# Two steps instead of three for a pair of attention heads, and both halves of the sample's scores at once

## The chip, the cores and the metric

The kernel runs as one program on one core of one Trainium2 chip. The metric is the time of one execution on the device in microseconds (us); the median of three runs of the kernel before is 1309.05 us (1308.57 to 1309.22). Engines are named as in the profile: PE is the matrix engine with its weight loads (PEld) beside it, DVE the vector engine, ACT the scalar engine with its function table, POOL the general engine, and SP the engine from whose queue the kernel starts its DMA transfers. PSUM is the memory that PE writes to; the other engines read it from there.

## The reference

One inference step of a two-layer encoder with a prompt of 512 frames (the rows 0 to 511) and a sample request of 32 frames (rows 512 to 543) that share the weights. Cut to what the change touches, with the shapes of this case (d_model 1024, 8 attention heads of 64, past of 256):

```python
def layer(x, ...):
    u = x @ w_in                       # 13 groups of columns: q, k, v, z of attention, of retention, ...
    # prompt: each chunk of 64 frames reads itself and the 8 chunks before it
    ya = band_attention_prompt(qa, ka, va, rel_table)
    # sample: 32 frames read 256 cached keys and their own 32
    ya = band_attention_sample(qa, ka, va, k_cache, v_cache, rel_table)
    ya = ya * silu(za)
    yb = group_norm_heads(retention(rope(qb), rope(kb), vb, ...)) * silu(zb)
    yc = rg_lru(xr, ...) * silu(zc)
    merged = sum(sigmoid(g_b) * (y_b @ w_branch[b]) for b in (A, B, C))
    r = ALPHA * x + merged @ w_out
    r = r + sigmoid(r @ w_ple_gate) * (pe @ w_ple)
    return layer_norm(r)

# both attentions, per head
scores = q * d**-0.5 @ k.T + rel_bias        # masked to the band for the prompt
probs = softmax(scores)
out = probs @ v
```

Since 8 chunks of 64 frames are the whole prompt but one chunk, a frame of the prompt reads all chunks up to its own: the scores of the four query tiles of 128 frames (i = 0 to 3) are 128, 256, 384 and 512 columns wide.

## The kernel before, in words

**The stream of blocks.** Activations lie with features on partitions and the 544 frames along the free axis. All large products are made of blocks: a 128x128 piece of a weight matrix against 544 frames, in two spans of 288 and 256 columns, and three times over, since both factors are split into a high and a low part (`xh`, `xl`, `wh`, `wl`); a block is so six matmuls at L256. Eight blocks (or four, or two) make a unit: an output tile, in one of two buffers of two PSUM banks each, that an evacuation (`evac`, lines 840 to 940) then copies or combines. A layer has 752 blocks, in the order of `layer_units()`: among others xr, va, then qa and ka in turn, kb, vb, qb, then za and what follows. Weights are loaded in chunks of eight blocks (`wr`, 3 buffers) and split into parts for four blocks at a time by ACT (`wh`, L211) and DVE (`wl`, L212), eight blocks ahead.

**What sets the order.** Everything else runs in generators, called jobs. `tick()` is called once ahead of each block; it issues the split that is due and then resumes every job whose time has come. A job says with `yield n` after how many blocks it wants to go on; these numbers stand in the table `PACE`. So the order of instructions on every engine is fixed when the program is built, and each engine and each DMA queue runs its list in order. If an instruction on PE waits for another engine, all blocks behind it wait with it.

**Attention of the prompt.** Once `ka` of head pair 0 is there, `attn_job` goes through the four pairs of heads. For a pair, three steps are added, 8 blocks apart: query tiles (0, 1), (2,) and (3,). A step (`attn_step`, L394 and on) takes the two buffers "sc" of PSUM (one bank of 512 columns each), one for each head j of the pair, and makes the scores by three products for each head and tile (high by high, low by high, high by low; L407). `exps` (L355 to L359) adds the bias and finds the row's extreme on DVE, takes the exponential on ACT with the row's sum; `norm` (L363, L364) multiplies by the reciprocal on DVE. Head 0's exponentials are issued with the scores, head 1's three blocks later together with head 0's norms, head 1's norms another three blocks later, and the transposes of head 0 two more (L423, by a matmul with the identity, 128 columns each, into the one "tp" bank); ACT copies them into `PT` (L429). Head 1's transposes follow three blocks behind. The product with V of a pair (`attn_pv`, L441, eight matmuls, in the one "pv" bank) is kept in a list and made by `flush()` right behind the first transposes of the next pair's step (0, 1); the last one comes `attn_end` = 9 blocks after the last step's slot. These pieces lie among the blocks of qa, ka, kb and vb.

**The sample.** `sample_job` starts behind `ka` of the last pair: it loads its cache and its biases `sb` (by SP, eight transfers), waits for "ya" (which stands from the first attention step on), and then 11 blocks. For j = 0 it makes scores (four matmuls at L468, 32 rows each at its own place in one bank), then exps; four blocks later the same for j = 1; the norms another four blocks later; then after four blocks the three transposes of j = 0 in the "tp" bank and two copies, and three blocks later those of j = 1; then three blocks later the product with V (L494).

**Behind attention.** `ret_job` starts once attention, the sample and the last tile of kb are there. It first turns VB (`flip`, L334: four transposes into "tp", then a copy), then KB, piece by piece. VB's tile t = 3 is copied out of PSUM by ACT (L866) at the end of its unit.

## Time and profile before

| what | value |
|---|---|
| median of the three runs | 1309.05 us (1308.57 to 1309.22) |
| profiled execution: time, span | 1308.99 us, 1307.2 us |
| granted PE clock in it | 0.997 of full speed |
| PE busy | 1290.2 us, 99% of the span |
| DVE, ACT, POOL busy | 719.6, 547.0, 176.3 us |
| PE on the chain that ended last | 95% of the span |

The profiled execution lies 0.06 us under the median. The span is the time from the first to the last recorded instruction; 1.8 us of the execution lie around it. In rows of the timeline the columns are: start in us from the span's start, length in us, engine, source line, operation, output and inputs, sizes and types, how many alike in a row, and in brackets the idle time of the engine before it with what ended it. "x2" behind a 288-column matmul stands for the pair of spans, 288 and 256.

### The profile page before, as it was taken

The page shows a single profiled execution, that of the slowest core. Times are in us where ns is not written, and L with a number is a line of the kernel's source. Part 1 is how long each engine was busy: PE and PEld are TensorE (multiplying, and loading weights), DVE is VectorE, ACT ScalarE, POOL GpSimd, SP SyncE. Part 2 cuts the span into 40 slices and gives each one's busy share as a digit, 9 for nine tenths or more (in the row PEclk, how much of TensorE's full clock was granted, in tenths as well). Part 3 has the DMA queues.
Part 4 walks back from the last instruction along what each step waited for, and adds up shares of the span by engine and source line. Part 5 has one row for each costly group of instructions (what it writes and reads, how often), then busy time and mean ns, then how long its engine had stood idle before and what let it go on. Part 6 is the DMA issues. An engine that isn't in the chain of part 4 may idle for free.

```text
span 1307.2 us, 25090 instructions
## 1 busy us (share of the span) xinstructions
PE 1290.2 (99%) x10552; PEld 1255.8 (96%) x10552; DVE 719.6 (55%) x1273; ACT 547.0 (42%) x1083; POOL 176.3 (13%) x158
## 2 busy tenths in 40 slices
PE   9999999999999999999999999999999999999996
PEld 9999889999999999999989998999999999999996
DVE  5666663563754443455584756626637534434567
ACT  6665544323632233323277655443235322332231
POOL 0210121410101101000032102125001011010000
PEclk9999999999999999999999999999999999999998
DMA  7333522321222222434132335222212222224231
GB/s 285 132 131 98 174 66 83 96 92 51 96 81 82 98 80 82 165 101 143 65 112 72 130 99 166 74 83 89 87 62 81 98 81 89 90 82 166 81 114 69
DMA packets 44609, 134.80 MB, mean 103 GB/s; under 512 B 9488, under 2 KB 11792, under 8 KB 42704
## 3 DMA queue, kind: packets, MB, share of 16 engines
q1 hardware_dynamic: 44496, 133.20, 30.6%
q8 instruction: 83, 1.36, 0.5%
q14 instruction: 30, 0.25, 0.1%
HBM read 117.02 MB, written 11.70 MB: 98 GB/s over the span
## 4 chain that ended last, share of the span: by engine, by line
PE 95%; DVE 3%; DMA 1%; ACT 1%; issue 0%; SPq 0%; POOL 0%; DVEq 0%
PE mm L256 84%; PE sc L407 2%; PE pv L441 1%; PE tp L423 1%; PE tp L334 1%; DMA raw<-in_W 1%; PE sc L667 1%; PE pv L690 1%; PE pv L522 0%; DVE r L819 0%; PE sc L522 0%; DVE xl L265 0%; PE sc L750 0%; PE sc L603 0%; PE pv L685 0%; PE sc L494 0%
## 5 line engine op out<-in xcount | busy, mean ns | idle before, releaser
L256 PE MATMUL mm<-xh,wh 128*128 128x288 f32 x2144 | 455.5, 294 | 0.4 <-ACT xrp L900 0.4
L256 PE MATMUL mm<-xh,wl 128*128 128x288 f32 x2144 | 444.2, 288 | 0.0
L256 PE MATMUL mm<-xl,wh 128*128 128x288 f32 x2144 | 442.8, 288 | 0.0
L212 DVE TENSOR_TENSOR wl<-raw,wh 128x512 fp32r<-128x512 f32 (+1 forms) x354 | 262.6, 760 | 282.3 <-ACT wh L211 277.2
L256 PEld LDWEIGHTS mm<-xh,wh 128*128 128x128 f32 x2144 | 328.4, 189 | 10.8 <-issue 7.5
L256 PEld LDWEIGHTS mm<-xl,wh 128*128 128x128 f32 x2144 | 328.8, 188 | 0.0
L256 PEld LDWEIGHTS mm<-xh,wl 128*128 128x128 f32 x2144 | 328.6, 188 | 0.0
L211 ACT CAST wh<-raw 128x512 fp32r<-128x512 f32 (+1 forms) x354 | 208.2, 614 | 36.0 <-PE mm L256 30.8
L922 ACT ACTIVATE sg<-mm 128x544 f32<-128x544 f32 x48 | 30.0, 625 | 154.0 <-PE mm L256 154.0
L934 POOL TENSOR_TENSOR m<-m,sg 128x544 f32<-128x544 f32 x30 | 46.8, 1561 | 316.7 <-DVE sg L932 316.7
L359 ACT ACTIVATE sx<-sx,sst 128x128 f32<-128x128 f32 (+4 forms) x68 | 38.0, 559 | 67.1 <-DVE sst L357 60.2
L256 PE MATMUL mm<-xh,held 128*128 128x288 f32 (+1 forms) x320 | 64.1, 292 | 0.3 <-ACT ple L942 0.3
L256 PE MATMUL mm<-mh,wh 128*128 128x288 f32 (+1 forms) x256 | 53.0, 288 | 0.0
L256 PE MATMUL mm<-mh,wl 128*128 128x288 f32 (+1 forms) x256 | 53.0, 288 | 0.0
L256 PE MATMUL mm<-ml,wh 128*128 128x288 f32 (+1 forms) x256 | 52.8, 287 | 0.0
L256 PEld LDWEIGHTS mm<-xh,held 128*128 128x128 f32 x320 | 51.3, 188 | 0.6 <-ACT ple L942 0.5
L256 PE MATMUL mm<-xl,held 128*128 128x288 f32 (+1 forms) x160 | 46.4, 290 | 0.6 <-DVE xl L265 0.6
L264 ACT CAST xh<-r 128x544 fp32r<-128x544 f32 (+2 forms) x32 | 17.0, 532 | 68.3 <-DVE r L952 64.1
L932 DVE TENSOR_TENSOR sg<-mm,sg 128x544 f32<-128x544 f32 x32 | 23.2, 725 | 37.0 <-PE mm L256 37.0
L913 ACT ACTIVATE z<-mm 128x544 f32<-128x544 f32 x24 | 15.0, 626 | 60.6 <-PE mm L256 60.5
L571 POOL TENSOR_TENSOR swap<-swap,cst 128x544 f32<-128x544 f32 x16 | 24.9, 1554 | 108.3 <-DMA swap<-QB 32.1
L256 PEld LDWEIGHTS mm<-mh,wh 128*128 128x128 f32 x256 | 39.4, 189 | 0.0
(251 smaller groups left out, 1783.4 us busy)
## 6 DMA issues: line engine op xcount, KB each, us to landing
raw<-in_W SPq DMA_DIRECT2D x189, 512.0 KB, 3.3
pled<-ple SPq DMA_DIRECT2D x4, 1088.0 KB, 9.8
ple<-pled SPq DMA_DIRECT2D x4, 1088.0 KB, 7.0
bias<-in_RB SPq DMA_DIRECT2D x16, 256.0 KB, 3.7
x<-in_xT SPq DMA_DIRECT2D x4, 544.0 KB, 9.5
o_v<-VA SPq DMA_DIRECT2D x2, 1088.0 KB, 4.6
o_k<-KT SPq DMA_DIRECT2D x2, 1088.0 KB, 5.1
swap<-KB SPq DMA_DIRECT2D x32, 68.0 KB, 2.0
```

The source lines that it names most:

```text
L211: S.copy(h[:, k:k + step], t)
L212: V.tensor_tensor(lo[:, k:k + step], t, h[:, k:k + step].bitcast(F32), SUB)
L256: T.matmul(ps[:, MM0 + a:MM0 + b], lhsT=w[:, n % 4, :], rhs=x[:, a:b], start=first and i == 0, stop=last and i == 2)
L264: S.copy(h, src)
L334: T.transpose(tp[:rows, t * 128:(t + 1) * 128], src[:, t, c0:c0 + rows], ident)
L359: S.activation(x, x, AF.Exp, bias=s[:, 0:1], scale=-1.0, accum_out=s[:, 1:2])
L407: T.matmul(scs[j][:, o:o + n], lhsT=q_[r, p, i * 128:i * 128 + 128], rhs=k_[r, p, :n], start=k == 0, stop=k == 2)
L571: G.tensor_tensor(sw, sw, cst[:, C_SIN:C_SIN + N], MUL)
L913: S.activation(z, pv, AF.Sigmoid)
L922: S.activation(sg, pv, AF.Sigmoid)
L932: V.tensor_tensor(sg, pv, sg, MUL)
L934: (V if kind == "bB" and t == 7 else G).tensor_tensor(m, m, sg, ADD)
```

## The change

**Attention.** A pair of heads takes two steps instead of three. The first ("wide") holds query tiles 3 and 1: tile 3's scores (512 columns) in the two "sc" banks as before, tile 1's (256 columns) in the "tp" bank for head 0 and in the "pv" bank for head 1. After the exponentials tile 1 of both heads lies side by side in a third buffer `x`. The second ("narrow") holds tiles 2 and 0, 384 and 128 columns, together in a head's "sc" bank. The wide step turns three full buffers with four transposes each (head 0's tile 3, head 1's tile 3, then tile 1 of both), the narrow one two; a wide step copies the first two with one instruction each, the third with two. `flush()` stands behind the wide step's first transposes. `PACE["step"]` becomes (11, 13), so that a pair still takes 24 blocks, and `attn_end` 3.

**The sample.** The loads of `sb` are moved behind the wait for "ya" and 14 blocks, with 12 blocks to the scores. Both halves' scores are made at once, in the two "sc" banks. All six transposes follow in one place, in two new "sc" banks: the four full ones in one, the two of 32 rows in the other; two copies take them out instead of four.

```diff
-    "va0": 5, "va": 3, "step": 8, "attn_end": 9, "at1": 3, "at2": 2, "at3": 3, "sample": 11, "sa1": 4, "sa2": 4,
+    "va0": 5, "va": 3, "step": (11, 13), "attn_end": 3, "at1": 3, "at2": 2, "at3": 3, "sample": 14, "sa1": 4, "sa2": 4,
...
-                for qs in ((0, 1), (2,), (3,)):
-                    if qs[0] == 2 and p < 3:
+                for n, qs in enumerate(((3, 1), (2, 0))):
+                    if n and p < 3:
                         bias_loads(p + 1)
                     add(attn_step(p, qs))
-                    yield PACE["step"]
+                    yield PACE["step"][n]
...
-            scs, xs, todo = [psum("sc") for _ in range(2)], [], []
-            o = 0
+
+            wide = qs[0] == 3
+            scs, xs = [psum("sc") for _ in range(2)], [tmp("sx", (128, 512)) for _ in range(2)]
+            at_ = {(qs[0], j): (scs[j], xs[j], 0) for j in range(2)}
+            if wide:
+                x = tmp("sx", (128, 512))
+                at_.update({(qs[1], j): (psum(("tp", "pv")[j]), x, 256 * j) for j in range(2)})
+            else:
+                at_.update({(qs[1], j): (scs[j], xs[j], 128 * (qs[0] + 1)) for j in range(2)})
...
-                        T.matmul(scs[j][:, o:o + n], lhsT=q_[r, p, i * 128:i * 128 + 128], rhs=k_[r, p, :n],
+                        sc, x, o = at_[i, j]
+                        o *= not wide
+                        T.matmul(sc[:, o:o + n], lhsT=q_[r, p, i * 128:i * 128 + 128], rhs=k_[r, p, :n],
                                  start=k == 0, stop=k == 2)
...
-            for j in range(2):
+            for x in xs + ([at_[1, 0][1]] if wide else []):
                 tp = psum("tp")
-                for c in range(0, o, 128):
-                    T.transpose(tp[:, c:c + 128], xs[j][:, c:c + 128], ident)
-
-                if j == 0 and qs[0] == 0:
+                mine = sorted((o, i, j) for (i, j), (_, y, o) in at_.items() if y is x)
+                end = mine[-1][0] + 128 * (mine[-1][1] + 1)
+                for c in range(0, end, 128):
+                    T.transpose(tp[:, c:c + 128], x[:, c:c + 128], ident)
+
+                if wide and x is xs[0]:
                     flush()
...
         def sample_job():
             ks, vc = sample_loads()
+            while "ya" not in env:
+                yield 2
+            yield PACE["sample"]
             sb = [tmp("sb", (128, PAST + NS)) for _ in range(2)]
...
-            while "ya" not in env:
-                yield 2
-            yield PACE["sample"]
+            yield 12
             xs = []
+            scs = [psum("sc") for _ in range(2)]
...
-            pts = []
+
+            tps = psum("sc"), psum("sc")
             for j in range(2):
                 x = xs[j][0]
-                tp = psum("tp")
                 for kt in range(3):
                     rows = 128 if kt < 2 else NS
-                    T.transpose(tp[:rows, kt * 128:(kt + 1) * 128], x[:, kt * 128:kt * 128 + rows], ident)
-                x = tmp("PT", (128, 384))
-                copy("pt")(x[:, :256], tp[:, :256])
-                copy("pt")(x[:NS, 256:], tp[:NS, 256:384])
-                pts.append(x)
-                yield PACE["sa3"]
+                    o = 256 * j + 128 * kt if kt < 2 else 128 * j
+                    T.transpose(tps[kt // 2][:rows, o:o + 128], x[:, kt * 128:kt * 128 + rows], ident)
+            pts = tmp("PT", (128, 512)), tmp("PT", (128, 512))
+            copy("pt")(pts[0], tps[0])
+            copy("pt")(pts[1][:NS, :256], tps[1][:NS, :256])
+            yield PACE["sa3"]
```

**Where instructions now stand.** Blocks are counted from the start of a layer, from 0. The scores of a pair stood at blocks 105, 113 and 121 (pair 0; the others 24, 48 and 72 later), and stand at 105 and 116. The transposes of pair 0 stood at 113 and 116, 121 and 124, 129 and 132; now at 113, 116 and 119, 124 and 127. The product with V of pairs 0 to 2 stays behind the transposes at 137, 161 and 185, where scores followed it directly and none do now; the last one moves from 209 to 203. The sample's scores stood at 155 and 159, now at 170; its transposes at 167 and 170, now at 182; its product with V at 173, now at 185. The turning of VB starts at 208 instead of 210.

ACT in layer 0, from the exponentials of pair 0's head 1 on (`sx` are exponentials, `sst` their sums, `PT` the turned probabilities). Before:

```order
L359 ACTIVATE sx,sst<-sx,sst 128x128 [waits DVE_49]
L359 ACTIVATE sx,sst<-sx,sst 128x256 [waits DVE_49]
L866 COPY KT<-mm 128x544 [waits PE_49]
L264 CAST KTh<-KT 128x544 [waits Activation_49]
L211 CAST wh<-raw 128x512 [waits DMAHW7_49]
L429 COPY PT<-tp 128x128 [waits PE_49]
L429 COPY PT<-tp 128x2x128
```

Now:

```order
L359 ACTIVATE sx,sst<-sx,sst 128x512 [waits DVE_49]
L359 ACTIVATE sx,sst<-sx,sst 128x256 [waits DVE_49]
L878 COPY KT<-mm 128x544 [waits PE_49]
L264 CAST KTh<-KT 128x544 [waits Activation_49]
L211 CAST wh<-raw 128x512 [waits DMAHW7_49]
L439 COPY PT<-tp 128x4x128 [waits PE_49]
L211 CAST wh<-raw 128x512
L439 COPY PT<-tp 128x4x128 [waits DMAHW5_49,PE_49]
```

The list between the exponentials and the first copy is the same; the exponentials are of 512 and 256 columns instead of 128 and 256, and the copies of four tiles. PE's second transposes, into the one "tp" bank, come behind the first copy in both.

DVE in layer 0 around the first scores of pair 3, where the sample's exponentials and norms are (the sums `sst_2156` and `sst_2204` and the buffers `sx_2155` and `sx_2203` are the sample's, `sst_2307` is that of pair 3's head 1, and the `KB` rows are the rotation of kb). Now:

```order
L357 ISA sx_2203,sst_2204<-sc_2146,sb_1960 128x288
...
L582 TENSOR_TENSOR KB_1868<-KB_1868,cst_90 128x544
L212 TENSOR_TENSOR wl_2231<-raw_1935,wh_2230 128x512
L357 ISA sx_2249,sst_2266<-sc_2247,bias_2032 128x512
...
L357 ISA sx_2251,sst_2269<-tp_2252,bias_2032 128x256
...
L364 TENSOR_SCALAR sx_2155<-sx_2155,sst_2156 128x288
...
L364 TENSOR_SCALAR sx_2203<-sx_2203,sst_2204 128x288
L585 TENSOR_TENSOR KB_1868<-KB_1868,swap_2128 128x544
L212 TENSOR_TENSOR wl_2298<-raw_1935,wh_2297 128x512
...
L364 TENSOR_SCALAR sx_2249<-sx_2249,sst_2266 128x512
...
L364 TENSOR_SCALAR sx_2251<-sx_2251,sst_2269 128x256
L357 ISA sx_2250,sst_2307<-sc_2248,bias_2034 128x512
```

Before, the sample's part was over by then:

```order
L498 COPY ya_1209<-sc_2218 128x4x32
L570 TENSOR_TENSOR KB_1870<-KB_1870,cst_90 128x544
...
L212 TENSOR_TENSOR wl_2269<-raw_1949,wh_2268 128x512
L357 ISA sx_2293,sst_2307<-sc_2291,bias_2012 128x128
...
L357 ISA sx_2293,sst_2310<-sc_2291,bias_2012 128x256
...
L573 TENSOR_TENSOR KB_1870<-KB_1870,swap_2139 128x544
L212 TENSOR_TENSOR wl_2335<-raw_1949,wh_2334 128x512
...
L364 TENSOR_SCALAR sx_2293<-sx_2293,sst_2307 128x128
...
L364 TENSOR_SCALAR sx_2293<-sx_2293,sst_2310 128x256
L357 ISA sx_2294,sst_2350<-sc_2292,bias_2014 128x128
```

Lines of "..." stand for sums, reciprocals and rows of a single column. The sample's norms now stand between head 0's exponentials and head 1's. On PE the sample's transposes stand five blocks behind pair 3's first scores; the third of them writes the second "sc" bank, which held head 1's scores, and so comes behind the last DVE row shown.

PE at the end of VB's unit, now:

```order
L256 MATMUL mm_2585<-xh_102,wl_2541 128x288
L256 MATMUL mm_2585<-xh_102,wl_2541 128x256
L334 MATMUL tp_2662<-cst_90,VB_2355 128x128 [waits PE_49]
L334 MATMUL tp_2662<-cst_90,VB_2355 128x128
L334 MATMUL tp_2662<-cst_90,VB_2355 128x128 [waits Activation_49] x2
L256 MATMUL mm_2655<-xh_101,wh_2586 128x288 [waits PE_49]
```

Here `mm_2585` is VB's tile t = 3, whose copy by ACT the last of the four transposes reads. Before, two blocks of the next unit and the product with V of pair 3 lay between, and the same transposes came in the middle of the unit behind:

```order
L441 MATMUL pv_2666<-PT_1210,vatok_1031 64x128
L441 MATMUL pv_2666<-PT_1211,vatok_1031 64x128
L256 MATMUL mm_2655<-xh_101,wh_2584 128x288
...
L256 MATMUL mm_2655<-xh_101,wl_2585 128x288
L256 MATMUL mm_2655<-xh_101,wl_2585 128x256
L334 MATMUL tp_2684<-cst_90,VB_2386 128x128 [waits PE_49]
L334 MATMUL tp_2684<-cst_90,VB_2386 128x128 x2
L334 MATMUL tp_2684<-cst_90,VB_2386 128x128 [waits Activation_49]
```

The turning of VB has moved from two blocks behind its last tile to right behind it.

More of the change, by code (lines that the diff above doesn't have):

```diff
@@ L406, in attn_step @@
                         r = slice(64 * j, 64 * j + 64)
-                        T.matmul(scs[j][:, o:o + n], lhsT=q_[r, p, i * 128:i * 128 + 128], rhs=k_[r, p, :n],
+                        sc, x, o = at_[i, j]
+                        o *= not wide
+                        T.matmul(sc[:, o:o + n], lhsT=q_[r, p, i * 128:i * 128 + 128], rhs=k_[r, p, :n],
                                  start=k == 0, stop=k == 2)
                 for j in range(2):
-                    now[j].append((xs[j][:, o:o + n], scs[j][:, o:o + n], env["bias", p, j][:, 512 - n:]))
-                o += n
+                    sc, x, o = at_[i, j]
+                    c = 0 if wide else o
+                    now[j].append((x[:, o:o + n], sc[:, c:c + n], env["bias", p, j][:, 512 - n:]))
+            todo = []
             for j in range(2):
@@ L419, in attn_step @@
             yield PACE["at2"]
-            for j in range(2):
+            for x in xs + ([at_[1, 0][1]] if wide else []):
                 tp = psum("tp")
-                for c in range(0, o, 128):
-                    T.transpose(tp[:, c:c + 128], xs[j][:, c:c + 128], ident)
-                if j == 0 and qs[0] == 0:
+                mine = sorted((o, i, j) for (i, j), (_, y, o) in at_.items() if y is x)
[3 more added lines that the diff above has]
+                if wide and x is xs[0]:
                     flush()
-                c = 0
-                for i in qs:
+                for c, i, j in mine:
                     copy("p%d" % j)(env["PT"][j][:, :i + 1, i * 128:i * 128 + 128],
                                     tp[:, c:c + 128 * (i + 1)].rearrange("p (a b) -> p a b", b=128))
-                    c += 128 * (i + 1)
+                if not wide and x is xs[1]:
+                    env["pvs"].append(lambda: attn_pv(p))
                 yield PACE["at3"]
-            if qs[-1] == 3:
-                env["pvs"].append(lambda: attn_pv(p))
         def attn_pv(p):
```

8 lines of the change are left out of this document (4 added, 4 removed).

## The prediction

> **What bounds the kernel now.** I read the page's totals and its chain of waits first:
>
> ```profile
> PE 1290.2 (99%) x10552; PEld 1255.8 (96%) x10552; DVE 719.6 (55%) x1273; ACT 547.0 (42%) x1083; POOL 176.3 (13%) x158
> PE 95%; DVE 3%; DMA 1%; ACT 1%; issue 0%; SPq 0%; POOL 0%; DVEq 0%
> ```
>
> PE is busy throughout and is 95% of the chain. A change on another engine is worth something only where PE waits for it, or no longer does. Next, what PE waits for (columns: tile and line, what ended the wait, us in all, how many, the longest):
>
> ```profile
> PE tp L750 <- DVE r L968: 2.0, 2, 1.4
> ```
>
> This largest one lies in the norm at a layer's end; none of attention is in that list. So no wait in attention can be saved. What can be saved is PE's own time at the seams, where it leaves the stream of blocks and comes back:
>
> ```profile
> 94.69 0.41 PE L256 MATMUL mm<-xh,wl 128*128 128x288 f32 x2
> 95.03 0.33 PE L407 MATMUL sc<-KTh,QTh 64*128 64x128 f32 x2
> 95.19 0.28 PE L407 MATMUL sc<-KTh,QTl 64*128 64x128 f32 x2
> 95.31 0.27 PE L407 MATMUL sc<-KTl,QTh 64*128 64x128 f32 x2
> ...
> 96.28 0.41 PE L256 MATMUL mm<-xl,wh 128*128 128x288 f32 x2
> ...
> 205.49 0.41 PE L256 MATMUL mm<-xh,wl 128*128 128x288 f32 x2
> 206.24 0.41 PE L256 MATMUL mm<-xh,wl 128*128 128x288 f32 x2
> 206.59 2.37 PE L441 MATMUL pv<-PT,vatok 128*64 128x512 f32 x16
> 208.89 0.52 PE L256 MATMUL mm<-xh,wh 128*128 128x288 f32 x2
> 209.25 0.41 PE L256 MATMUL mm<-xl,wh 128*128 128x288 f32 x2
> ```
>
> Two like pairs of spans a block apart start at 205.49 and 206.24: a block takes 0.75 us, a pair 0.25. A seam's cost is the distance from the last pair ahead of it to the second pair behind it, less two pairs: for the step (0, 1), 96.28 - 94.69 - 0.50 = 1.09 us; for the product with V 209.25 - 206.24 - 0.50 = 2.51. From a seam's first start to the second pair behind it is 0.15 us more than the cost (1.25 and 2.66); I take that off below. Going out (94.69 to 95.03) takes 0.34 us from start to start and coming back (208.89 to 209.25) 0.36, where the stream has 0.25: a visit costs some 0.2 us of nothing but switching, so fewer visits are the gain to be had.
>
> **The change part by part. Fewer seams.** The other steps before:
>
> ```profile
> 109.85 0.49 PE L423 MATMUL tp<-cst,sx 128*128 128x128 f32 x3
> 110.27 0.50 PE L407 MATMUL sc<-KTh,QTh 64*128 64x512 f32 x2
> 110.61 0.39 PE L407 MATMUL sc<-KTh,QTl 64*128 64x512 f32 x2
> 110.84 0.40 PE L407 MATMUL sc<-KTl,QTh 64*128 64x512 f32 x2
> ...
> 111.52 0.41 PE L256 MATMUL mm<-xl,wh 128*128 128x288 f32 x2
> 126.05 2.37 PE L441 MATMUL pv<-PT,vatok 128*64 128x512 f32 x16
> ...
> 128.63 0.34 PE L407 MATMUL sc<-KTh,QTl 64*128 64x384 f32 x2
> 128.81 0.33 PE L407 MATMUL sc<-KTl,QTh 64*128 64x384 f32 x2
> ...
> 129.43 0.42 PE L256 MATMUL mm<-xl,wh 128*128 128x288 f32 x2
> 146.45 0.69 PE L468 MATMUL sc<-kvc,qs 64*32 64x288 f32 x8
> 147.42 0.42 PE L256 MATMUL mm<-xl,wh 128*128 128x288 f32 x2
> ```
>
> Step (3,): 111.52 - 110.27 - 0.15 = 1.10. Step (2,) behind the product with V adds 129.43 - 126.05 - 2.66 = 0.72; standing alone (pair 0) it is 1.10 less three passes of 128 columns, each 0.05 shorter (starts 0.18 instead of 0.23 apart), so 0.94. A pair's scores cost 1.09 + 0.94 + 1.10 = 3.13 in pair 0 and 1.09 + 0.72 + 1.10 = 2.91 in the other three: 11.86 a layer. After: the wide step is 1.10 plus three passes of 256 columns, the narrow one 0.94 plus three of 128. Such short passes start 0.12 apart: 1.46 and 1.30, times four 11.04. That saves 0.82. The transposes are as many as before (80 a layer) and take at most 0.14 each (three of them from 109.85 to 110.27), some 0.11 within a group; the product with V stays 2.51. The sample's scores cost 147.42 - 146.45 - 0.15 = 0.82 a half; for both at once, between 0.82 (the halves use different rows of PE) and 1.07 (one more pair's time); I take 0.95: 0.7 saved. Sum: 1.5 us a layer, **3.0 in all**.
>
> ACT's four copies fewer, and the same counts on DVE, POOL and SP, are worth nothing by themselves: PE waits for none of these now. What counts is whether it will wait, since its list is in order and a block behind a wait is late by all of it. I looked for three places.
>
> **A. The second transposes of pair 0 (block 116).** There is one "tp" bank: they wait for ACT's copy of the first. Before:
>
> ```profile
> 99.35 1.86 DVE L212 TENSOR_TENSOR wl<-raw,wh 128x512 fp32r<-128x512 f32 x1 [0.25 <-ACT wh L211]
> 101.98 0.28 DVE L357 CUSTOM_DVE_ANT_0 sx<-sc,bias 128x128 f32<-128x128 f32 x1
> ...
> 103.20 0.59 ACT L866 COPY KT<-mm 128x544 f32<-128x544 f32 x1
> ...
> 104.89 0.53 ACT L429 COPY PT<-tp 128x128 f32<-128x128 f32 x2
> 105.75 0.49 PE L423 MATMUL tp<-cst,sx 128*128 128x128 f32 x3
> 113.02 0.68 DVE L357 CUSTOM_DVE_ANT_0 sx<-sc,bias 128x512 f32<-128x512 f32 x1
> 113.75 0.72 ACT L359 ACTIVATE sx<-sx,sst 128x512 f32<-128x512 f32 x1 [0.99 <-DVE sst L357]
> ```
>
> DVE's chain is as before up to `wl`'s end at 101.2. Two norms of 128 and 256 columns with their reciprocals filled the 0.77 to 101.98; with 512 and 256 I take 1.05. Head 1's op, of 512 columns now (0.68 with the overlap of its neighbours, 0.6 from start to start), so ends near 102.9. ACT's exponentials of 512 (0.72) and 256 (some 0.5) end near 104.2, where KT's copy began at 103.20: 1.0 later. The same rows follow up to the copy `PT`, two instructions then and one of four tiles now; it was done near 105.4, so 106.4. PE used to come at 105.75, after a step (2,); without that (-0.94, up to -1.1 as it is next to transposes there), with a wide step for the step (0, 1) (+0.37) and one more transpose (+0.11) it comes at 105.1 to 105.3; I take 105.2. A wait of 1.2 us. In layer 1 the same chain starts earlier against PE: there
>
> ```profile
> 752.70 0.53 ACT L429 COPY PT<-tp 128x128 f32<-128x128 f32 x2
> 754.04 0.49 PE L423 MATMUL tp<-cst,sx 128*128 128x128 f32 x3
> ```
>
> the copy done near 753.2 moves to 754.15, PE from 754.04 to 753.7: 0.4. Bounds for both layers: 0.6 if DVE and ACT run some tenths faster than their rows, 2.4 if the longer chain also meets layer 1's scans. I take **1.6**.
>
> **B. The sample's transposes (block 182).** They are five blocks behind pair 3's wide step, and the third needs the "sc" bank that DVE reads last, for head 1's exponentials. PE is there at 1.46 + five blocks + two transposes = 5.45 us after pair 3's first score. DVE's work on the way, in rows of before around that score (174.42 us):
>
> ```profile
> 157.18 0.37 DVE L364 TENSOR_SCALAR sx<-sx,sst 128x288 f32<-128x288 f32 x1
> 158.58 0.68 DVE L212 TENSOR_TENSOR wl<-raw,wh 128x512 fp32r<-128x512 f32 x1
> 175.52 0.29 DVE L357 CUSTOM_DVE_ANT_0 sx<-sc,bias 128x128 f32<-128x128 f32 x1 [0.33 <-PE sc L407]
> 176.88 1.29 POOL L576 TENSOR_TENSOR KB<-KB,cst 128x512 f32<-128x512 f32 x1 [7.36 <-DVE KB L573]
> 178.83 1.41 DVE L364 TENSOR_SCALAR sx<-sx,sst 128x128 f32<-128x128 f32 x1
> 178.79 1.36 POOL L571 TENSOR_TENSOR swap<-swap,cst 128x544 f32<-128x544 f32 x1
> ```
>
> From the first score: DVE starts at 1.1 (175.52), has head 0's two ops (512 and 256 columns) by 2.05, the sample's two norms with reciprocals (0.47 each, of it 0.37 the norm) by 3.0, KB's addition by 3.65 (a like op takes 0.68 at 158.58), `wl` by 4.3. Then come head 0's norms and head 1's op, 1.7 us when nothing is in the way: 6.0, a wait of 0.55. But POOL multiplies KB right behind the addition (176.88, released by it), and the next `swap` behind that (178.79). There DVE's norm of 128 columns took 1.41 us and ended together with POOL's instruction; the op of 128 columns at 175.52 took 0.29, and one of 288 columns 0.37. Two such meetings, one per POOL instruction, put head 1's op at 7.95: a wait of 2.5. One meeting gives 1.4. I take 2.0 a layer, nearer the blocked end, since both POOL rows follow from DVE's own order: **4.0**, bounds 1.1 and 5.0.
>
> [...]
>
> **C. Turning VB at its unit's end (block 208).** The fourth transpose reads tile 3, which ACT copies only then:
>
> ```profile
> 205.94 0.61 ACT L866 COPY VB<-mm 128x544 f32<-128x544 f32 x1 [2.44 <-PE mm L256]
> ```
>
> The unit's last pair started at 205.49, the copy ended at 206.55, 1.06 later. The transposes come 0.25 after that pair and the fourth 0.33 later: at 0.58. A wait of 0.5 a layer, **1.0** in all; before, two blocks covered it. It is the surest of the three, 0.8 to 1.2.
>
> Covered: tile 1's "tp" bank is freed by ACT two blocks ahead, the "pv" bank by DVE 0.5 to 1 us ahead of the product with V, and the sample's scores come 0 to 2 us after their banks are free. These I take at nothing; if DVE is half a microsecond later there, each of some ten places costs up to that.
>
> Sum: -3.0 + 1.6 + 4.0 + 1.0 = +3.6 on 1308.99 us: 1312.6, and 0.06 more against the median: **1312.6**.
>
> **The rivals.** *About no change:* POOL lets DVE through at the sample. Then B is 1.1 to 2.8, and the sum +0.7 to +2.4: 1309.7 to 1311.4. For it: DVE's ops before POOL's start may get ahead in layer 1, whose chain stands otherwise. Against: the addition that starts POOL stands ahead of head 1's op in DVE's own list. *Faster:* PE arrives everywhere after its data; only the 3.0 show: 1306.0, or 1307.0 with C alone. It is decided at block 182: if head 1's op ends by 5.4 us after pair 3's first score. For it: DVE is idle 45% of the time. Against: even the unblocked list ends at 6.0. *Worse:* the sample's eight loads of `sb` now stand in SP's queue in the middle of attention and wait for a free buffer; KB's `swap` transfers, queued behind them, come late and with them the rotation that DVE and POOL share. At 0.5 us for each of eight further stops, +4: 1316.6. Against: SP's transfers are few there. *The change does not save seams*, because a visit's cost is columns, not switching: 3.0 becomes about 1, and the time 1314.6; the 0.2 less of a score behind a product with V speaks against it.
>
> **How the numbers follow.** Forecast 0.46; about no change 0.33; faster 0.10; worse 0.06; no seams saved 0.05. One execution of this kernel can't be told from another within 0.2%, 2.6 us: 1306.4 to 1311.7. Slower by more takes the forecast, worse and no seams: 0.57 less a little of the forecast's lower edge, 0.55; faster by more is part of the case "faster": 0.09; the rest, 0.36, is the same. Range: from the edge of the faster case with half a wait, 1307.8, to the sum with every wait at its upper bound (-3.0 + 2.4 + 5.0 + 1.2 = +5.6) and a little of "worse", 1315.5. The forecast's own range is 1311.0 to 1315.0.
>
> **What would show it.** The seams: wide steps of about 1.46 and narrow ones of 1.30 from first start to the stream, the sample's scores in one visit. Among PE's waits, which have no row of attention now, three new ones: "tp" at the second transposes of pair 0 put down to ACT's copy `PT`, about 1.2 and 0.4; the sample's transposes "sc" put down to DVE's `sx` or `sst`, about 2 each; "tp" of VB put down to ACT's VB copy, 0.5 each. The forecast is wrong if the sample's transposes follow the block ahead without a gap, or if a gap appears where none is named.

## The result and the profile after

The changed kernel takes 1317.48 us, the median of six executions (1315.57 to 1319.42); the kernel before, on the same chips, 1308.65. The ratio is 1.0068, with a 95% interval of 1.0055 to 1.0081: 0.7% slower. The forecast was slower, at 1312.6 us with a range up to 1315.5; the sign was right, the size less than half of it.

The profiled execution is one of the faster ones, 1315.92 us with a span of 1314.1 us, against 1307.2 before: 6.9 us more. The page's totals and its chain of waits, after:

```profile
span 1314.1 us, 25065 instructions
PE 1288.7 (98%) x10552; PEld 1257.1 (96%) x10552; DVE 710.8 (54%) x1273; ACT 543.0 (41%) x1079; POOL 175.5 (13%) x158
PE 82%; DVE 10%; ACT 4%; issue 2%; DMA 1%; DVEq 0%; POOL 0%; SPq 0%; ACTq 0%
```

PE is busy 1.5 us less, and the span is 6.9 us longer. On the chain of waits PE's share fell from 95% to 82%, and DVE and ACT, 4% together before, now hold 14%. What PE waits for, by tile (us in all, times, longest); the rows that were not there before:

```profile
PE sc L493 <- DVE sst L357: 5.2, 2, 2.6
PE mm L256 <- ACT wh L211: 1.8, 2, 0.9
PE tp L434 <- ACT PT L439: 1.3, 2, 0.7
PE tp L334 <- ACT VB L878: 0.7, 2, 0.4
```

Three of the four were named ahead: the sample's transposes (5.2 of wait), pair 0's second transposes (1.3), VB's turning (0.7). The second row was not: PE waits for split weights, far behind attention. Each comes twice, once a layer.

**The seams**, by the same reckoning as in the prediction (the stream's own time taken off). A wide step, a narrow step behind transposes, and the sample's scores, after:

```profile
118.25 0.42 PE L256 MATMUL mm<-xh,wl 128*128 128x288 f32 x2
118.60 0.50 PE L414 MATMUL sc<-KTh,QTh 64*128 64x512 f32 x2
...
120.21 0.41 PE L256 MATMUL mm<-xl,wh 128*128 128x288 f32 x2
130.92 0.41 PE L256 MATMUL mm<-xh,wl 128*128 128x288 f32 x2
131.17 0.60 PE L434 MATMUL tp<-cst,sx 128*128 128x128 f32 x4
131.70 0.45 PE L414 MATMUL sc<-KTh,QTh 64*128 64x384 f32 x2
...
133.06 0.41 PE L256 MATMUL mm<-xl,wh 128*128 128x288 f32 x2
162.96 0.41 PE L256 MATMUL mm<-xh,wl 128*128 128x288 f32 x2
163.30 0.71 PE L478 MATMUL sc<-kvc,qs 64*32 64x288 f32 x16
...
164.30 0.41 PE L256 MATMUL mm<-xl,wh 128*128 128x288 f32 x2
```

The wide step costs 120.21 - 118.25 - 0.50 = 1.46, as predicted. Four transposes and a narrow step cost 133.06 - 130.92 - 0.50 = 1.64; the transposes alone are 0.44, so the scores 1.20 (predicted 1.30). The sample's sixteen score matmuls cost 164.30 - 162.96 - 0.50 = 0.84, no more than eight did before (0.82): a seam of 0.8 is saved whole.

**The sample's transposes.** PE, DVE and POOL around block 182 of layer 0; pair 3's first score is at 170.29:

```profile
174.14 1.76 POOL L588 TENSOR_TENSOR KB<-KB,cst 128x512 f32<-128x512 f32 x1 [3.72 <-DVE KB L585]
174.87 1.31 DVE L364 TENSOR_SCALAR sx<-sx,sst 128x512 f32<-128x512 f32 x1
176.25 1.32 POOL L583 TENSOR_TENSOR swap<-swap,cst 128x544 f32<-128x544 f32 x1
176.29 1.44 DVE L364 TENSOR_SCALAR sx<-sx,sst 128x256 f32<-128x256 f32 x1
177.64 0.68 DVE L357 CUSTOM_DVE_ANT_0 sx<-sc,bias 128x512 f32<-128x512 f32 x1
175.41 0.38 PE L493 MATMUL sc<-cst,sx 128*128 128x128 f32 x2
178.39 0.61 PE L493 MATMUL sc<-cst,sx 128*32 128x128 f32 x4 [2.60 <-DVE sst L357]
```

Both norms run beside a POOL instruction, and take 1.31 and 1.44 us for 512 and 256 columns. Head 1's op ends at 178.25 (its next row), 7.96 us after the first score. This is the blocked end of the prediction (7.95), not the middle that it took. Layer 1 has the same to 0.02 us.

**Behind attention.** ACT at the end of retention's first products: before, then after; and PE at the first blocks that read zc's result (`zch`, `zcl`), after:

```profile
244.74 0.37 ACT L606 COPY kvs<-sc 128x256 f32<-128x256 f32 x1 [3.54 <-POOL QB L577]
245.13 1.28 ACT L913 ACT_TABLE_LOAD   x1
246.42 0.62 ACT L913 ACTIVATE z<-mm 128x544 f32<-128x544 f32 x1
```

```profile
248.11 1.28 ACT L925 ACT_TABLE_LOAD   x1 [2.87 <-PE mm L256]
249.40 0.62 ACT L925 ACTIVATE z<-mm 128x544 f32<-128x544 f32 x1
...
272.12 0.41 PE L256 MATMUL mm<-xh,wl 128*128 128x288 f32 x2
273.42 0.52 PE L256 MATMUL mm<-zch,wh 128*128 128x288 f32 x2 [0.89 <-ACT wh L211]
273.78 0.41 PE L256 MATMUL mm<-zcl,wh 128*128 128x288 f32 x2
274.26 0.52 PE L256 MATMUL mm<-zch,wl 128*128 128x288 f32 x2
```

A pair starts 0.25 us behind the one before in the stream; at the first product with `zch` it is 1.30 us (272.12 to 273.42), and the two pairs behind it take 0.36 and 0.48. How much that is in all, the distance between two seams of retention tells, with 58 blocks between them in both kernels; before, and after:

```profile
229.34 0.74 PE L603 MATMUL sc<-vbtok,kbtok 128*64 128x64 f32 x18
...
276.47 0.59 PE L656 MATMUL sc<-QB,KB 64*32 64x32 f32 x16
```

```profile
229.51 0.57 PE L615 MATMUL sc<-vbtok,kbtok 128*64 128x64 f32 x12
...
278.48 0.40 PE L668 MATMUL sc<-QB,KB 64*32 64x32 f32 x9
```

47.13 us before, 48.97 after: 1.84 us lost, and in layer 1 the same to 0.03. The other new thing in these rows is ACT's load of its function table: before, it ran directly behind a copy (245.13), while PE was still at work; now ACT is idle for 2.87 us, waits for PE, and only then loads.

**Does it add up?** By the same reckoning, all that PE's stream loses from the first scores to retention's first products, waits included, is 41.4 and 41.3 us in the two layers before and 43.4 and 43.5 after: 4.1 more in all. Pair 0 has 0.80 and 0.92 of it (1.7), the sample's transposes 2.74 and 2.78 (5.5), VB's turning 0.60 and 0.59 (1.2). So fewer seams save 4.3: 0.8 a layer on the sample's scores, 1.4 and 1.3 on attention's. The zc blocks come behind that stretch and cost 1.84 a layer (3.7). -4.3 + 1.7 + 5.5 + 1.2 + 3.7 = +7.8, and the span has +6.9; most of the rest lies in stretches that the change doesn't touch, which are shorter in this execution (attention starts 0.16 us earlier, and from retention to the next layer it is 0.6 less). Between the medians it is 8.8, 1.9 more than between the spans: the profiled execution lies 1.6 under its median, the one before 0.3 above its own. The six executions are 1315.6, 1315.9, 1317.4, 1317.5, 1319.1 and 1319.4, three groups some 1.8 us apart.

### The profile page after: what moved, and what is told of

It reads as the page before. It is cut to its first block, busy times and chain, and to the rows that moved or that the text cites. A ratio compares the mean times of both kernels' runs of the same rounds, so it can differ in the third digit from the quotient of the medians.

```text
span 1314.1 us, 25065 instructions
## 1 busy us (share of the span) xinstructions
PE 1288.7 (98%) x10552; PEld 1257.1 (96%) x10552; DVE 710.8 (54%) x1273; ACT 543.0 (41%) x1079; POOL 175.5 (13%) x158
## 4 chain that ended last, share of the span: by engine, by line
PE 82%; DVE 10%; ACT 4%; issue 2%; DMA 1%; DVEq 0%; POOL 0%; SPq 0%; ACTq 0%
PE mm L256 73%; DVE wl L212 2%; PE pv L450 1%; PE tp L434 1%; DMA raw<-in_W 1%; PE sc L414 1%; PE sc L679 1%; PE tp L334 1%; PE pv L702 1%; DVE lru_i L567 1%; ACT wh L211 1%; DVE sx L357 1%; PE pv L534 0%; DVE z L930 0%; PE sc L534 0%
## 5 line engine op out<-in xcount | busy, mean ns | idle before, releaser
L359 ACT ACTIVATE sx<-sx,sst 128x512 f32<-128x512 f32 (+2 forms) x68 | 37.7, 557 | 46.1 <-DVE sst L357 34.6
L439 ACT COPY PT<-tp 128x384 f32<-128x384 f32 (+2 forms) x64 | 24.9, 428 | 43.9 <-PE tp L434 37.0
L256 PEld LDWEIGHTS mm<-ml,wh 128*128 128x128 f32 x256 | 39.3, 188 | 0.0
```

The costliest lines, as they stand in the source:

```text
L256: T.matmul(ps[:, MM0 + a:MM0 + b], lhsT=w[:, n % 4, :], rhs=x[:, a:b], start=first and i == 0, stop=last and i == 2)
L359: S.activation(x, x, AF.Exp, bias=s[:, 0:1], scale=-1.0, accum_out=s[:, 1:2])
L439: copy("p%d" % j)(env["PT"][j][:, :i + 1, i * 128:i * 128 + 128], tp[:, c:c + 128 * (i + 1)].rearrange("p (a b) -> p a b", b=128))
```

## The experiments

**What varies between executions.** The changed kernel itself, unedited.

> The changed kernel once more, to see what varies between its executions: six of them took 1315.6, 1315.9, 1317.4, 1317.5, 1319.1 and 1319.4 us, and only the 1315.9 was profiled. If one event of some 1.8 us happens in neither, one or both layers, times fall in three groups again and a slower profile has a wait that the first lacks, in one layer or both. If it is jitter, times are spread evenly and no wait changes by more than some tenths.

Five executions took 1315.93 to 1319.24 us, and the profiled one was the longest, with a span of 1317.5. Its waits are those of the first profile but for 0.3 us in pair 0. Stretches around the sample's wait in layer 0 (columns: stretch, length, busy time and count of PE, its loads, DVE, ACT, POOL, then the granted PE clock, DMA share and GB/s), in this execution and then in the first profiled one:

```profile
176.20:179.61 3.41, 0.81 (x8) 0.56 (x7) 3.38 (x8) 0.52 (x1) 2.05 (x3) 1.00 0.48 154
179.62:183.02 3.40, 3.40 (x17) 3.40 (x16) 1.40 (x5) 1.50 (x6) 0.00 (x0) 0.50 0.00 0
```

```profile
173.55:176.96 3.41, 2.24 (x19) 2.00 (x17) 3.33 (x6) 0.48 (x1) 2.82 (x3) 1.00 0.42 120
176.97:180.37 3.40, 1.98 (x17) 1.98 (x18) 3.33 (x10) 1.96 (x6) 0.60 (x1) 1.00 0.12 47
180.38:183.79 3.41, 3.41 (x58) 2.93 (x57) 0.03 (x1) 0.43 (x2) 0.00 (x0) 1.00 0.00 0
```

Behind the wait of 2.6 us PE's clock is granted at half for 3.41 us, and the same stands behind the wait in layer 1 (831.56 to 834.97). From the third of the sample's transposes to the next scores PE needs 12.46 us in layer 0 and 12.23 in layer 1, where the first profile has 10.94 and 10.93: an event costs 1.5 and 1.3 us. With 0.3 us in pair 0 that is most of the 3.4 us between the two spans. One event a layer, in neither, one or both, so accounts for most of the spread; neither and both are profiled in this kernel, a single one in the next run. The jitter theory falls. The five new times do not stand in groups as clear as the first six.

Why a wait of the same length was followed by half clock in one execution and not in the other, the traces let one see. In this execution the clock switches at 179.61, 183.03, 831.56 and 834.97, which lie 1, 190 and 1 steps of 3.413 us apart. In the profile before, full clock is on record from 5.31 to 1298.96 us, in the first profile after from 6.30 to 1306.78: 379.0 and 381.0 such steps. On this grid lie the stretches in the rows above. In this execution the whole wait falls into one step, where PE is busy for 0.81 of 3.41 us; in the first profile a step's edge at 176.97 cuts the same wait, and PE is idle for 1.17 us of one step and 1.42 of the next. Of the 760 steps at full clock in the profiles before and after, all but the last of each hold at most 1.42 us of idle PE, and full clock follows; the two last, at the kernels' end, hold 2.44 and 2.98, and half clock follows. So between these two executions the place of the edges made the difference. Where between 1.42 and 1.74 us (the least idle time that a row or run here shows with half clock behind it, below with the sample at 160) the change comes, is not shown.

**Retention two blocks later.** Does moving retention bring the waits for weights?

```diff
-                    add(ret_job())
+                    add(ret_job(), 3)
```

> The changed kernel with retention's job added two blocks later, so that VB is turned at block 210 as before the change. Theory: the waits behind attention (VB's fourth transpose 0.6 us a layer, and the waits for split weights among the blocks of zc, about 1.5 us a layer, which are seen in the profile after and not in that before) come from retention standing two blocks earlier. Then both go, the span falls from 1314.1 by 4.2 to about 1310, and PE's waits for ACT's wh are gone. Rival: the weights are late because of transfers or the changed middle of attention; then only VB's 1.2 go, and the waits for wh stay.

1314.87 us (ratio 1.0047, 1.0035 to 1.0060), span 1312.3 with a stretch of half clock in layer 0 that costs 1.5 us (12.43 from the third transpose to the next scores instead of 10.94). VB's wait is gone. The waits for wh are not:

```profile
PE mm L256 <- ACT wh L211: 0.7, 2, 0.3
```

Between the two seams of retention 1.06 us of the 1.84 stay (48.19), although from block 210 on ACT, DVE and POOL now have the same list of instructions as before the change. Each theory was half right, so I looked for where the same list runs later. Against PE, DVE is 1.3 us late from zc's first tile on, because ACT's sigmoid is, because of the table's load:

```profile
249.36 1.28 ACT L925 ACT_TABLE_LOAD   x1 [1.36 <-PE mm L256]
250.65 0.62 ACT L925 ACTIVATE z<-mm 128x544 f32<-128x544 f32 x1
```

The built programs tell why it waits. Before the change:

```
L606 COPY kvs<-sc 128x256 [waits DMAHW5_49,DMAHW4_49,DMAHW6_49,PE_49,Pool_49]
L913 ACT_TABLE_LOAD
L913 ACTIVATE z<-mm 128x544 [waits PE_49]
```

and after:

```
L618 COPY kvs<-sc 128x256 [waits PE_49]
L925 ACT_TABLE_LOAD [waits DMAHW5_49,DMAHW4_49,DMAHW6_49,PE_49]
L925 ACTIVATE z<-mm 128x544 [waits Pool_49]
```

The tmp pool's 14 buffers are given out in turn, and the changed steps take fewer of them (20 a layer for scores instead of 24). Before, z got the buffer of an attention tile, which PE had read last, and the buffer of a `swap` tile went to `kvs`, whose copy carried the waits. Now z gets the one that held a `swap` tile, written by DMA and worked on by POOL. All these waits and the one for PE belong to the sigmoid; all but one stand on the table's load ahead of it. By the trace PE's was the last to be fulfilled: ACT's 2.87 us of idle time ahead of the load are put down to it.

**An extra tile ahead of z.** This shifts the turn by one, so z gets an attention tile's buffer again.

```diff
+                if kind == "zc" and t == 0:
+                    V.memset(tmp("pad", (128, 8)), 0.0)
                 z = tmp("z")
```

> The changed kernel with one small extra tile of the tmp pool, set by DVE just ahead of the first tile of zc, so that this tile's z takes the next buffer of the pool. In the changed kernel z reuses a buffer that a swap transfer and POOL used last, and the load of ACT's function table ahead of its sigmoid carries the waits for them and for PE, so its 1.28 us start only when PE is done; before, the buffer was an attention tile's and the load ran ahead of the wait. Theory: this late load is most of what makes the split weights late among zc's blocks (1.5 us a layer); with the load ahead again, the waits for wh fall to 0 to 0.5 us a layer and the span from 1314.1 to 1311 to 1312 where the clock stays full. Rival: retention's two blocks are the cause; then the waits for wh stay near 1.5 us a layer.

1315.45 us (1.0057, 1.0045 to 1.0069). The span, 1314.4, has two stretches of half clock in it (mean granted clock 0.995, against 0.997), so it can't be set against 1314.1; the waits can. There is no row of PE waiting for wh any more, and between the seams of retention, at full clock, 0.64 us a layer is left of 1.84 (47.76). The load is ahead of the wait again:

```profile
247.10 1.28 ACT L927 ACT_TABLE_LOAD   x1
249.92 0.63 ACT L927 ACTIVATE z<-mm 128x544 f32<-128x544 f32 x1 [1.53 <-PE mm L256]
```

Undoing the load alone gives 1.20 of the 1.84 back, undoing retention's move alone 0.78: together 1.98, so if the two are all of the 1.84 they hardly hide one another.

**Both together.**

> The extra tile and retention two blocks later together. Theory of two causes: the two blocks alone left 0.7 us a layer of the waits for wh; with the table's load ahead too none is left, DVE's chain through zc stands against PE as before the change, and VB's wait is gone as well: 1314.1 - 2.9 - 1.2 = 1310 of span where the clock stays full. Rival: something third (transfers, the order of the jobs); then some 0.7 us a layer of waits for wh stays.

1311.18 us (1.0030, 1.0021 to 1.0039), span 1308.6 at full clock. The distance between the seams is 47.13 again, to the hundredth that of before; that is 3.7 in all where the expectation had 2.9, pair 0 is 0.2 shorter here and the start 0.25, and so the span lies 1.4 under the expected 1310. Eight of its eleven executions lie between 1310.4 and 1312.2, the others reach 1317.25: the sample's wait of 2.6 us is still in it, and may halve the clock there as above, though none of the three was profiled.

**POOL or DVE's list.** The changed kernel without POOL's multiplication of KB by the decay factors, one of the two instructions beside the norms; retention's keys lack these factors here.

```diff
+            if key == "qb":
-            G.tensor_tensor(e, e, bc(w, [[0, 4], [1, 128]]), MUL)
-            G.tensor_tensor(a[:, NP:], a[:, NP:], w[:, :NS], MUL)
+                G.tensor_tensor(e, e, bc(w, [[0, 4], [1, 128]]), MUL)
+                G.tensor_tensor(a[:, NP:], a[:, NP:], w[:, :NS], MUL)
```

> The changed kernel without POOL's multiplication of KB by the decay factors (so retention's keys lack them); POOL's multiplication of the swapped halves stays. Theory: DVE's two norms of 512 and 256 columns took 1.31 and 1.44 us instead of 0.49 and 0.35 because POOL's two instructions run at the same time; with one of the two gone, one norm is as short as alone and the sample's wait falls from 2.6 to 1.2 to 1.8 us a layer. Rival: the wait is the length of DVE's list alone; then it stays above 2.3 and both norms stay long.

1314.63 us (1.0046, 1.0033 to 1.0059). DVE, POOL and PE's wait:

```profile
175.34 0.49 DVE L364 TENSOR_SCALAR sx<-sx,sst 128x512 f32<-128x512 f32 x1
175.94 1.24 DVE L364 TENSOR_SCALAR sx<-sx,sst 128x256 f32<-128x256 f32 x1
175.53 1.50 POOL L583 TENSOR_TENSOR swap<-swap,cst 128x544 f32<-128x544 f32 x1 [5.61 <-DMA swap<-KB]
```

```profile
PE sc L493 <- DVE sst L357: 3.2, 2, 1.6
```

The norm of 512 columns takes 0.49 with no POOL instruction beside it; the one of 256 still meets the `swap` and takes 1.24. The wait falls from 2.6 to 1.6, as the theory had it. The five executions lie within 1.0 us (1314.24 to 1315.25), and in the profiled one nothing halves the clock. Its span is 1313.5, only 0.6 less than that of the first profile, though the sample's waits are 2.0 less: it is the longest of the five, and pair 0's waits are 0.6 longer in it (1.9 instead of 1.3).

**The sample 12 blocks earlier.**

```diff
-"sample": 14
+"sample": 2
```

> The changed kernel with the sample 12 blocks earlier: scores at block 158, transposes at 170 with no wide step's scores shortly ahead. Theory: the sample's wait of 2.6 us a layer comes from standing five blocks behind a wide step whose head 1 reads the bank last; then most of it goes, 4 to 5 us of the span in all, to about 1309.5. Rival: wherever it stands, the second bank is read late by the step ahead (here the narrow one, three blocks ahead of the transposes); then 1 us or more a layer stays and the span is 1311 or more.

1312.20 us (1.0029, 1.0018 to 1.0040), seven executions within 1.1 us; span 1310.1, 4.0 less. The transposes' wait is gone altogether (their seam is 0.66). What was expected and didn't come is 0.9 us a layer: at block 158 the scores cost 1.72 instead of 0.84. The second half of them waits for the bank that the wide step's head 1 is read from, two blocks ahead, and the two halves no longer run side by side. It is a wait for a bank again (put down to DVE's `sst`, with 0.22 us of idle PE), only at a new place.

**The three repairs together.**

> The extra tile, retention two blocks later and the sample 12 blocks earlier. If the four causes add up, the sample alone (1310.1) less the 4.1 of the waits behind attention: a span of 1306.0, 1.2 under that of before, with only the wait in pair 0 left (0.7 us a layer), and no stretch of halved clock. If the causes hide one another, the span stays at 1307.5 or more.

1307.37 us (0.9998, 0.9989 to 1.0006), span 1305.5 against the 1306.0 expected: they add up. The change now costs nothing, but gains nothing that can be measured either. Three of the eleven executions took 1309.0 to 1310.5; why, no profile shows.

**Pair 0, first try.** The transposes of its wide step two blocks later, and the narrow step's scores too, with its exponentials drawn together so that its transposes stay at 124.

```diff
-                    yield PACE["step"][n]
+                    yield PACE["step"][n] + (2, -2)[n] * (p == 0)
...
-                yield PACE["at1"]
+                yield PACE["at1"] - (p == 0 and not wide)
...
-            yield PACE["at2"]
+            yield PACE["at2"] + 2 * (wide and p == 0)
```

> As the one before, and in pair 0 the wide step's transposes two blocks later (115, 118, 121, the narrow step's scores at 118, its transposes where they were). Theory: the wait for ACT's copy in pair 0 is the length of ACT's list ahead of it against PE, and 1.5 us of blocks cover it: 1.4 us less in all, a span near 1304.6. Rival: ACT's copies come later with it; then the wait of 0.7 a layer stays.

1313.48 us (1.0040, 1.0026 to 1.0055): 6 us worse. The wait at the second transposes did go, as expected; a larger one of 2.5 us came at the narrow step's transposes:

```profile
113.85 0.61 ACT L359 ACTIVATE sx<-sx,sst 128x384 f32<-128x384 f32 x1 [2.15 <-DVE sst L357]
...
114.85 0.62 ACT L439 COPY PT<-tp 128x256 f32<-128x256 f32 x2
...
115.52 1.11 PE L434 MATMUL tp<-cst,sx 128*128 128x128 f32 x4 [2.54 <-ACT PT L439]
```

My edit put head 1's exponentials on ACT ahead of the copy of the third tile, and behind an evacuation: the copy stood in line for them, and PE for the copy. The clock was halved behind it in both layers (granted at 0.50 from 116 to 118 us and at 0.52 from 767 to 769).

**Pair 0, second try.** Only the wide step's transposes later.

```diff
-            yield PACE["at2"]
+            yield PACE["at2"] + 2 * (wide and p == 0)
```

> As the kernel with three repairs (extra tile, retention two blocks later, sample 12 blocks earlier), and in pair 0 the wide step's transposes two blocks later (115, 118, 121), while the narrow step stays: scores at 116, transposes at 124 and 127, head 1's exponentials at 119, ahead of the evacuation at block 120. Theory: the run before this one got rid of the wait at pair 0's second transposes and lost 2.5 us at the narrow ones only because head 1's exponentials came behind that evacuation and ahead of the third copy on ACT. Then no wait of more than 0.3 us is left in pair 0, the narrow scores cost 0.1 to 0.2 us more alone, and the span falls from 1305.5 to 1304.4 +- 0.4. Rival: one of pair 0's transposes waits for ACT whatever their place; then the waits for PT stay above 0.5 us a layer and the span does not fall.

1306.67 us (0.9982, 0.9974 to 0.9991), eleven executions within 1.5 us; span 1304.5. This version beats both kernels: 0.2% under the one before, 0.8% under the changed one. Some 0.9 us of wait at pair 0's transposes is left in two places, more than the 0.3 expected; the span came out as the theory had it.

**The sample at 160.** One change to that version, "sample" from 2 to 4.

> The same and the sample two blocks later (scores at 160, transposes at 172). With the sample at 158 its scores' seam costs 1.71 us, where it cost 0.84 in the changed kernel: the banks are read until then by the wide step's head 1, two blocks ahead. Two blocks on, 0.84 again: 1.7 less in all, a span near 1302.8, and a time some 4 us under the kernel before. Rival: the seam at 158 is long for another reason (the transfers of sb); then it stays above 1.3.

1314.65 us (1.0042, 1.0029 to 1.0055), the median of five executions; a sixth took 2108 us at a mean granted clock of 0.609, and no profile shows why. The scores' seam is 0.84 as expected. But the sample's head 1 is now read at block 164, where the narrow step needs the bank, and the wait has only moved: 1.0 us at the narrow step's first transposes in layer 0 (0.5 in layer 1) and 1.3 at its scores. The clock is halved behind them in both layers, for 6.8 us each time, though neither wait alone is long: together they leave PE busy for 1.45 of 3.41 us in the one step of the clock's grid, and for 1.67 in layer 1:

```profile
157.57:160.98 3.41, 1.45 (x9) 0.80 (x7) 2.90 (x6) 1.62 (x4) 1.83 (x2) 1.00 0.21 82
160.99:167.81 6.82, 6.42 (x31) 6.31 (x32) 3.37 (x15) 2.19 (x7) 1.39 (x2) 0.50 0.25 79
```

**The sample at 159**, with "sa1" 3 and "sa2" 5 so that its second exponentials and its transposes stay.

> As the kernel of 1304.5 us of span (all repairs), with the sample's scores one block later (159), its second exponentials three instead of four blocks behind (162, as there) and its transposes where they were (170). There the scores' second half waited for the bank that DVE reads for the wide step's head 1, and the seam cost 1.72 us instead of 0.84. If that read is all it waits for, 0.75 us of a block covers it, the seam costs 0.85 to 1.0 and the span is 1303.0 +- 0.4. If the sample's exponentials then come late for the narrow step at 164, as they did with the scores at 160, a wait of 0.5 us or more a layer stands there and the span does not fall.

1307.41 us (0.9991, 0.9982 to 1.0000), span 1306.6. The scores' seam is 0.96, and then the transposes at 170 wait again (1.2 us in layer 0) and the narrow step 0.6. The second outcome, in part at another place than named: of the places tried between two steps (158, 159, 160) none is free of cost. Whether 158 or 159 is the better one is not shown, as the two intervals overlap.

**Attention alone.** The changed attention with the sample as it was before the change.

> The change of attention alone, with the sample as before the change. It has the wait in pair 0 (0.8), VB's (0.6), the late table load and retention two blocks earlier (1.5), each a layer, but no sample transposes behind a wide step. Saved are attention's seams alone, 1.3 us a layer. If the parts add up: 1307.2 + 2 * (0.8 + 0.6 + 1.5 - 1.3) = 1310.4 of span, no stretch of halved clock, and times within 1.5 us of each other. If the changed attention itself is what costs, the span is 1312 or more.

1314.00 us (1.0038, 1.0026 to 1.0050), executions within 1.2 us, no stretch of half clock; span 1311.9, 1.5 more than expected. Of this 1.2 is one row, at a place that I had not thought of: the old sample's transposes share "tp" with the narrow step's at block 170.

```profile
PE tp L434 <- ACT PT L493: 1.2, 2, 0.6
```

So attention's change alone costs 4.7 us of span at full clock. The 1.2 of that row the whole change doesn't have, as its sample takes no "tp" bank; the other 3.5 are half of its 6.9.

## Why the prediction was right and wrong

**What bounds the kernel**: right. Only PE's waits, its seams and its clock moved the end; ACT's four copies fewer bought nothing that shows.

**Fewer seams**: right in kind, too small. 3.0 was predicted and 4.3 measured. The wide step is 1.46 as priced. The narrow step was priced as a visit of its own, 1.30, but it stands behind transposes and needs no way out of the stream: 1.20, which is 0.4 less over the four pairs of a layer. Pair 0's step (2,) before was taken at 0.94; behind its transposes it took 1.12 in layer 0 and 0.93 in layer 1. And the sample's two halves run fully side by side, at the lower bound: sixteen matmuls cost 0.84 where eight cost 0.82.

**A, pair 0**: the mechanism was right. That the sum came so near (1.7 against 1.6) is partly luck: 0.8 and 0.9 were measured, not 1.2 and 0.4. In layer 1 the text let PE come 0.34 us earlier, where its own terms (-0.94 + 0.37 + 0.11) give 0.46; with that the wait there would have been some 0.6 and the sum 1.8.

**B, the sample's transposes**: the mechanism was right, and the experiment without POOL's multiplication confirms it. The size was not: 5.5 against 4.0, above even its upper bound of 5.0. Each wait alone is 2.6, where two meetings were priced at 2.5, and some 0.16 a layer are lost beside it. The step that failed is "One meeting gives 1.4. I take 2.0 a layer": the order on DVE made both meetings certain, and the text averaged over a doubt that no row supports. In the profile before, eight norms began beside one of POOL's long multiplications, and all eight ended only behind it, after 1.20 to 1.76 us instead of 0.29 to 0.49. Both meetings did happen here, with norms of 1.31 and 1.44 us.

**C, VB**: right, 1.2 against 1.0, and called the surest.

**What was left out**: here the prediction failed. At "I looked for three places" it counted retention's move by two blocks at its first instruction only, VB's turning, and put all that follows at nothing without a word. Everything that retention issues on DVE moved with it, up to sixty blocks on, and the pool's turn of buffers shifted by four a layer with the tiles that the steps no longer take. Together they made the weights late at zc: 3.7 us that stand in no term. With both undone this loss goes (47.13 between the seams, as before), with either one it goes in part.

**The clock**: missing as well. A wait was priced at its length. Behind one of 2.5 or 2.6 us PE ran at half clock in seven of twelve cases, at 1.3 to 1.5 us each for the sample's, which is most of the 1.6 us between the first profile and the median.

**What the named terms hide**: together they came to +4.1 (-4.3 + 1.7 + 5.5 + 1.2), near the forecast's +3.6. That is luck, since the seams saved 1.3 more and the sample's transposes cost 1.5 more than priced, and the two errors cancel. What took the time out of the range is the two terms without a name, zc's late weights and the clock.

**The rivals**: "about no change" needed POOL to let DVE through; the norms beside it took 1.31 and 1.44 us, so it didn't. "Faster" needed head 1's op to end by 5.4 us after the first score; it ended at 7.96. "Worse", at 1316.6, has the right size by the wrong cause: no wait for `swap` or `sb` is among PE's rows. "No seams saved" fell with the seams. The range's upper end was the sum of all named waits at their upper bounds, 1314.6, and a little; with the two unnamed terms beyond it, it could not hold the time.

In numbers: +3.6 predicted, +7.8 as the sum of the terms as measured, +6.9 in the span, +8.8 between the medians.

## What to carry to other kernels

Where a job moves by even two blocks, follow everything that it issues, on every engine, to its end, and not only the place where it starts. A changed number of tiles from a shared pool changes which buffer every later tile gets, and with it which waits it inherits; look at the waits of the built program before and after, above all on table loads. And where a change brings PE a wait as long as those that half clock followed here (one of 2.5 us, or two of 1.0 and 1.3 close together), price it with the slower clock behind it, and fix the longest wait before the many short ones.

## What the runs showed of the hardware

PE's clock is granted at full (1.00) or at half (0.50) in the stretches shown above. In these executions its switches lie whole steps of 3.413 us apart: 379.0 and 381.0 steps apart in the profiles before and after, 1, 190 and 1 in the repeated run. The place of the grid differs: an edge lies 1.90, 2.89 and 2.12 us behind the span's start in these three. In the profiles before and after, full clock followed every step with up to 1.42 us of idle PE, and half clock the two with 2.44 and 2.98. In the repeated run half clock followed a step with 2.60 us of idle, with the sample at 160 steps with 1.96 and 1.74. Twelve waits of 2.5 or 2.6 us were profiled, in six executions, and behind seven of them the clock fell to half. In the repeated run the sample's wait of layer 0 lay in one step; in the first profile, where none was followed by half clock, an edge cut it in both layers (1.17 and 1.42 us, 1.42 and 1.19). Two waits close together (1.0 and 1.3 us, and 0.5 and 1.3) did it too, for 6.8 us; why twice as long is open. At the half clock a pair of spans starts 0.45 us behind the one before instead of 0.25 (in the repeated run, from 179.43 on):

```profile
179.43 0.65 PE L256 MATMUL mm<-xh,wh 128*128 128x288 f32 x2
179.87 0.66 PE L256 MATMUL mm<-xl,wh 128*128 128x288 f32 x2
180.33 0.66 PE L256 MATMUL mm<-xh,wl 128*128 128x288 f32 x2
```

An event behind the sample's wait cost 1.3 to 1.5 us.

In the changed kernel's first profile DVE's norms beside POOL's multiplications took 1.31 to 1.40 us for 512 columns, where the others took 0.49, and 1.44 for 256, where the others took 0.35. They ended 0.28 to 0.29 and 0.15 us behind POOL's instruction.

Each of the 22 loads of ACT's function table in the profiles before and after takes 1.28 us. In the changed kernel the one at zc carries waits of the instruction behind it and starts only behind 2.87 us of idle ACT; before, it ran directly behind a copy that carried the waits. Which of the two happened depended on the buffer that the instruction writes, as the run with the extra tile shows (the load at 247.10, the sigmoid at 249.92), and nothing in the kernel's text tells it.
